# An encoder block on one core: output projection, norm 2 and feed-forward with features on the partitions and tokens along the free axis

## The chip, the cores and the metric

The kernel runs on one core of a Trainium2 chip. The metric is device time in microseconds (us) of one execution. The kernel before was run three times: median 1041.16 us, from 1040.82 to 1041.45. A profile of one execution shows what each engine did: TensorE (PE, and PEld for its weight loads), VectorE (DVE), ScalarE (ACT), GpSimd (POOL), and SyncE (SP), which issues most DMA transfers. Each engine works through its own queue in order; engines wait for each other through semaphores.

## What is computed

One layer of a transformer-like encoder on x of 1024 tokens by 1024 features, in float32:

```python
h = rms_norm(x, norm1_g)
z = h @ w_in
a, gate, q, k, v = jnp.split(z, splits, axis=-1)
conv_out = conformer_conv(a, gate, dw_kernel, dw_bias, conv_ln_g, conv_ln_b)
attn_out = neighbourhood_attention(rms_norm(q), rms_norm(k), v, rpb)
mix = jnp.concatenate([conv_out, attn_out], axis=-1)
x = x + mix @ w_out
h = rms_norm(x, norm2_g)
x = x + (jax.nn.silu(h @ w_gate) * (h @ w_up)) @ w_down
```

`w_out` is 1024 x 1024, `w_gate` and `w_up` are 1024 x 2816, `w_down` is 2816 x 1024. The tokens form a grid of 16 rows by 64 columns for the attention.

## The kernel before

A float32 product is made of three matmuls in a reduced format. `split` (L105) writes a high part with a cast on ACT (L106) and a low part, source less high part, on one or two engines that the caller names (L110: VectorE or POOL). `mac` (L112) then issues high by high, high by low, low by high. The first operand is the stationary one (the weight load, 128 by 128), the second the moving one (up to 512 columns).

*Weights of the output projection.* `want` lists the chunks, `issue` loads the next into one of three raw buffers (L148, tag R), `take` splits it (L151). `wo` comes as eight chunks of two 128-row blocks and 512 output features: wo04, wo06, wo00, wo02 for the first half of the features, wo14, wo16, wo10, wo12 for the second. All loads go through SP's queue in program order.

*Output projection.* `proj(t, d, acc, ks)` (L786) accumulates tile t of 128 tokens by half d of 512 output features over the eight blocks of the mixed features: blocks 4 to 7 come from attention (`at`), 0 to 3 from the convolution group (`cm`). The activations are stationary, the weights moving, so a result has tokens on the partitions and features along the free axis. After every `mac`, `weave` runs one piece of other work from the list `woven`. The first half of the features runs for tiles 0 to 5 in between the last attention blocks and the norm of the convolution group (L889 to L935), then for tiles 6 and 7 (L936 to L941). `take(2)` at L940 is where wo14 to wo12 are split. `resid` adds x to the result. The second half (L1204 to L1213) runs tile by tile; `norm2` stores the finished rows to the scratch `xd` in DRAM, sums the squares along the free axis with ACT (L948) and takes the root. One tile later `norm2_out` multiplies the rows by the reciprocal root and norm2_g (L956) into `xn`.

*From tokens to features.* The next products contract over features, so features must lie on the partitions. `t2_one` (L1198) transposes tokens 0 to 511 of `xn` with TensorE, four 128 x 128 transposes to a group (L1201), and splits the result into `h2`.

*Products with gate and up weights.* They are a Strassen-like scheme on 2 x 2 blocks: halves of the features and halves of the tokens on the left, pairs of weight blocks on the right. Seven products m1 to m7 stand in place of eight; `LEFT` (L1217) names the left operand of each: A11, A12, A22 are blocks of the normed x; S1 to S4 are sums of blocks, S1 = A21 + A22, S2 = S1 - A11, S3 = A11 - A21, S4 = A12 - S2. The left sums are made on the rows by `s_sum` (L1143), then transposed and split by `s_T` (L1157 to L1176), woven between the matmuls of the first products. A product is four `mac` of 512 columns for each of 22 pairs i of weight blocks (`product`, L1220); the weight sums are made by `t_sums` (L972), the operands by `prep` (L1106) and `part`. m1 and m2 accumulate in a bank A, m7 and m4 in D, m6, m5, m3 in B, and `evac` (L1237) reads a bank after each product, before the next product adds to it. Row pairs 0 and 1 run together, product by product, in the order of L984; the pairs from 2 on run in `ORDER` (L982). The results go to DRAM as operands of the next scheme (`keep`, L1269).

*Down products.* The seven products with `w_down` (L1437 to L1476) use the gated activations as the stationary operand and the weights as the moving one. `finish` adds the residual read back from `xd` (`load_res`, L1398) and `store` writes rows of the output.

Buffers: G tiles of 4 KB a partition (25), H tiles of 16 KB (6), R tiles for raw loads (3); PSUM has four banks `mm`, two `tp`, and `cv` of two banks.

## Time and profile before

| quantity | value |
|---|---|
| three runs, median (lowest to highest) | 1041.16 us (1040.82 to 1041.45) |
| the profiled execution, first to last instruction | 1039.2 us |
| mean granted TensorE clock | 0.999 |
| PE busy | 1033.1 us |
| DVE busy | 767.6 us |
| ACT busy | 477.5 us |
| POOL busy | 446.8 us |
| HBM read and written | 112.90 MB, 44.76 MB |

The span is that of one profiled execution; the runs' time also holds what lies around the first and last instruction. A row of the timeline has the start in us, the duration in us, engine, line, operation, out<-in by the program's names, the shape and a count; brackets at its end tell how long the engine sat idle before it and what ended that. SPq is a DMA issue on SP's queue. A row of the groups by tile has the number of instructions, then the shortest, the median and the longest duration in ns, and the first and last start. A row of the windows has the stretch and its length, then busy us and number of instructions for PE, PEld, DVE, ACT and POOL, the granted clock as a share of full speed, the DMA share and GB/s. The names in the rows leave buffer numbers out, so `t1m` is a weight operand of a product and `A`, `B`, `D` are the banks.

### The profile page before, as it was taken

What the parts mean: (1) busy time and instruction counts of PE and PEld (TensorE: products, weight loads), DVE (VectorE), ACT (ScalarE), POOL (GpSimd) and SP (SyncE); (2) the same over time, 40 slices, a digit from 0 to 9 for tenths busy, and PEclk for the clock granted to TensorE, in tenths of its full rate; (3) what the DMA queues carried; (4) which work ended last, traced back from release to release, by engine and by line L of the source; (5) the groups of instructions that cost most, each with busy time, mean ns of one, the idle gap of its engine ahead of it and who ended that gap; (6) DMA issues with size and microseconds to landing.
All of it is one profiled execution on the core that took longest, in us unless ns stands there. A gap on an engine that the chain in (4) does not pass through costs nothing.

```text
span 1039.2 us, 15251 instructions
## 1 busy us (share of the span) xinstructions
PE 1033.1 (99%) x5398; PEld 860.4 (83%) x5398; DVE 767.6 (74%) x1209; ACT 477.5 (46%) x1047; POOL 446.8 (43%) x351
## 2 busy tenths in 40 slices
PE   9999999999999999999999999999999999999998
PEld 7888888877777888888888888888888888888886
DVE  5788987886754257685888787787787767758884
ACT  7465348837866235434333334333342443433431
POOL 1036755524641302668776666667566200002310
PEclk9999999999999999999999999999999999999999
DMA  9426781247316422131434334424433597633741
GB/s 351 158 80 199 232 231 60 83 159 237 99 36 168 142 82 81 57 121 67 161 114 157 129 120 153 152 85 150 152 127 107 198 350 265 210 102 104 238 128 49
DMA packets 74077, 153.07 MB, mean 147 GB/s; under 512 B 13712, under 2 KB 22672, under 8 KB 73360
## 3 DMA queue, kind: packets, MB, share of 16 engines
q1 hardware_dynamic: 71984, 148.73, 43.3%
q10 hardware_dynamic: 2016, 3.35, 1.0%
q8 instruction: 43, 0.70, 0.3%
q14 instruction: 34, 0.28, 0.1%
HBM read 112.90 MB, written 44.76 MB: 152 GB/s over the span
## 4 chain that ended last, share of the span: by engine, by line
PE 98%; DVE 1%; ACT 1%; DMA 0%; issue 0%; DVEq 0%
PE B L114 6%; PE B L116 6%; PE B L115 6%; PE z L114 4%; PE z L115 4%; PE z L116 4%; PE D L114 4%; PE D L115 4%; PE D L116 4%; PE gl L116 3%; PE gl L114 3%; PE gl L115 3%; PE p L700 2%; PE o L719 2%; PE s L660 2%; PE pj L114 2%
## 5 line engine op out<-in xcount | busy, mean ns | idle before, releaser
L344 DVE SCALAR_TENSOR_TENSOR cv<-u,par,cv 128x1009 f32<-128x1009 f32 (+14 forms) x92 | 117.5, 1277 | 2.3
L370 POOL TENSOR_TENSOR pa<-pa,pr 128x1022 f32<-128x1022 f32 (+5 forms) x24 | 57.9, 2414 | 47.6 <-ACT pr L369 43.7
L106 ACT CAST op<-sr 128x512 fp32r<-128x512 f32 x77 | 47.7, 619 | 60.5 <-PE B2d L116 26.8
L1435 POOL TENSOR_TENSOR ou<-ou,resm 128x512 f32<-128x512 f32 x8 | 12.2, 1524 | 144.2 <-DMA resm<-xd 143.9
L110 DVE TENSOR_TENSOR op<-sr,op 128x512 fp32r<-128x512 f32 x77 | 59.3, 771 | 17.2 <-ACT op L106 17.2
L106 ACT CAST op<-wd 128x512 fp32r<-128x512 f32 x66 | 40.9, 619 | 29.9 <-DVE wd L1337 17.2
L689 POOL TENSOR_SCALAR e<-e,rs 128x288 f32<-128x288 f32 (+1 forms) x64 | 33.9, 545 | 42.0 <-DVE rs L687 41.8
L110 DVE TENSOR_TENSOR op<-wd,op 128x512 fp32r<-128x512 f32 x66 | 50.5, 765 | 1.5
L979 DVE TENSOR_TENSOR ts<-gu,ts 128x512 f32<-128x512 f32 x44 | 49.9, 1134 | 0.8
L678 ACT ACTIVATE e<-e,mx 128x288 f32<-128x288 f32 (+1 forms) x64 | 36.5, 571 | 18.8 <-DVE mx L673 18.8
L673 DVE CUSTOM_DVE_ANT_0 e<-s,tab 128x288 f32<-128x288 f32 (+1 forms) x64 | 28.7, 503 | 13.6 <-PE s L660 13.6
L1252 DVE TENSOR_TENSOR g<-D,g 128x512 f32<-128x512 f32 x22 | 15.2, 689 | 23.1 <-PE D L116 23.1
L1151 POOL TENSOR_TENSOR xn<-xn,xn 128x512 f32<-128x512 f32 x4 | 6.9, 1714 | 56.5 <-DVE sn L1151 50.9
L397 ACT ACTIVATE sq<-z,r 128x64 f32<-128x64 f32 x96 | 28.3, 329 | 4.5 <-PE z L116 4.5
L1259 ACT ACTIVATE D<-D 128x512 f32<-128x512 f32 x22 | 12.8, 582 | 35.8 <-DVE D L1258 35.8
L369 ACT ACTIVATE pr<-u,par 128x1022 f32<-128x1022 f32 (+5 forms) x24 | 27.0, 1137 | 1.6 <-ACT vs L427 1.6
L700 PEld LDWEIGHTS p<-ident,e 128*96 128x96 f32 (+1 forms) x192 | 20.6, 133 | 7.1 <-POOL e L689 6.3
L114 PE MATMUL B2d<-op 128*128 128x512 f32 x66 | 25.8, 391 | 0.0
L115 PE MATMUL B2d<-op 128*128 128x512 f32 x66 | 25.7, 389 | 0.0
L116 PE MATMUL B2d<-op 128*128 128x512 f32 x66 | 25.7, 389 | 0.0
L948 ACT ACTIVATE jk<-x 128x1024 f32<-128x1024 f32 x8 | 8.2, 1029 | 36.3 <-DVE x L841 36.3
L719 PE MATMUL o<-e,vw 96*64 96x128 f32 (+1 forms) x384 | 24.7, 277 | 0.0
(1479 smaller groups left out, 3748.7 us busy)
## 6 DMA issues: line engine op xcount, KB each, us to landing
gu<-in_gu SPq DMA_DIRECT2D x44, 512.0 KB
sr<-sd SPq DMA_DIRECT2D x77, 256.0 KB
sd<-sd SPq DMA_DIRECT2D x22, 512.0 KB
wd<-in_wd SPq DMA_DIRECT2D x44, 256.0 KB
sd<-g SPq DMA_DIRECT2D x33, 256.0 KB
x<-in_x SPq DMA_DIRECT2D x16, 512.0 KB
xd<-x SPq DMA_DIRECT2D x8, 512.0 KB
resm<-xd SPq DMA_DIRECT2D x16, 256.0 KB
```

Source lines behind the costliest of these rows:

```text
L106: act.copy(hi, src)
L110: eng.tensor_tensor(*[w[..., sl] for w in (lo, src, hi.bitcast(F32))], OP.subtract)
L114: pe.matmul(acc, lh, rh, start=start, stop=False, skip_group_check=True)
L115: pe.matmul(acc, lh, rl, start=False, stop=False, skip_group_check=True)
L116: pe.matmul(acc, ll, rh, start=False, stop=stop, skip_group_check=True)
L344: dve.scalar_tensor_tensor(acc[:, o], uc[:, i], dwk[:, c, t:t + 1], acc[:, o], OP.mult, OP.add)
L370: pool.tensor_tensor(pa[:, o], pa[:, o], pr[:, o], OP.add)
L678: act.activation(e, e, AF.Exp, bias=mx.pop((i, hh)), scale=-1.0, accum_out=sums[i][:, hh:hh + 1])
L689: pool.tensor_scalar(es[i][:, hh], es[i][:, hh], rs[:, hh:hh + 1], 1.0, op0=OP.mult, op1=OP.mult)
L700: pe.transpose(pt[:m, g * P:(g + 1) * P], es[i][:, hh, g * m:(g + 1) * m], ident)
L719: pe.matmul(os_[s_][hh * HD:(hh + 1) * HD, hp], vw[cb, rh + g][:, c:c + HD], pTs[i][hh][:, g], start=g == 0, stop=g == 2)
L979: dve.tensor_tensor(o, l, r, OP.subtract)
```

## The change

Everything from the output projection on has features on the partitions and tokens along the free axis.

- The host also lays out x as `xp`, features by tokens with the tokens in the order that the attention uses, and turns the output, now features by tokens, back. norm2_g becomes eight columns of `par`.
- `proj(m, h, ks, sel, every)` computes 128 output features m by 512 tokens h: weights stationary, activations moving. The first two units of the first token half run in two column pairs (`OUTER` and `INNER`), since the attention blocks finish in the order 0, 3, 1, 2. Units (0..3, 0) and (0..1, 1) come first, then (4..7, 0) and (2..7, 1).
- `at` lies in two H tiles; `wo` in pairs of G tiles except wo14 and wo16; some projection weights move from G to H; G has 21 tiles and H 7.
- `resid` adds x and stores to `xd` at once: sixteen stores of 256 KB in place of eight of 512 KB.
- Norm 2 sums over partitions: ACT squares each block, POOL adds the eight squares (`square`), TensorE multiplies by a column of ones (`token_sums`), ACT and VectorE take the root and the reciprocal, TensorE spreads it over partitions (`token_rows`), and VectorE scales each block in place (`norm2`).
- The transposes of `xn` and of the left sums go. `left` makes the left sums in place on the blocks, VectorE the sum, ACT the cast, POOL (for S2 VectorE) the low part. They are emitted after the products that the dictionary `after` names, and the order of the products of pairs 0 and 1 changes.
- For pairs 0 and 1, m4's gate and up steps follow m6 and m5 (`gate2`, `up2`). In the down products activations and weights change places.

The diff, cut to its core:

```diff
+        "xp": f["x"].reshape(2, 8, 4, 16, D).transpose(4, 0, 2, 3, 1).reshape(KB, P, S),
...
-        return T("G", [P, 1024], 25, name, dt)
+        return T("G", [P, 1024], 21, name, dt)
...
-        return T("H", [P, 4096], 6, name, dt)
+        return T("H", [P, 4096], 7, name, dt)
...
+            if (d, k0 // 4) == (1, 1):
+                if not woq:
+                    woq.append(H(f"wo{d}{k0}", F32R))
+                o = k0 % 4 * 1024
+                hl = (woq[0][:, o:o + 1024], woq[0][:, o + 1024:o + 2048])
+            else:
+                hl = (G(f"wo{d}{k0}h", F32R), G(f"wo{d}{k0}l", F32R))
...
+    xd = dr.tile([KB, P, S], F32, name="xd")
+    cm, xT, acc = [], {}, {}
+    OUTER, INNER = "outer", "inner"
+
+    def cols(w, sel):
+        if sel == OUTER:
+            return w.rearrange("p (b q) -> p b q", b=4)[:, 0:4:3]
+        return w[:, P:3 * P] if sel == INNER else w
+
+    def proj(m, h, ks, sel=None, every=1):
+        out = cols(acc[m, h], sel)
+        for n, k in enumerate(ks):
+            r = [cols((w[:, k] if k < 4 else w[:, k - 4])[:, h * 512:(h + 1) * 512], sel) for w in (cm if k < 4 else at)]
+            mac(out, [w[:, m % 4 * P:m % 4 * P + P] for w in wo[m // 4, k]], r, k == 4 and sel != INNER, k == 3)
+            if n % every == every - 1:
+                weave()
...
+    def load_xT(m):
+        xT[m] = G(f"xT{m}")
+        nc.sync.dma_start(xT[m], a["xp"][m])
+
+    def resid(m, h):
+        w = xT[m][:, h * 512:(h + 1) * 512]
+        dve.tensor_tensor(w, acc[m, h], w, OP.add)
+        nc.sync.dma_start(xd[m][:, h * 512:(h + 1) * 512], w)
+
+    def fill(m, *ks):
+        if not acc:
             act.activation(warm, eps, AF.Sqrt)
-            acc0.append(mm("pj0"))
-        proj(0, 0, acc0[0], ks)
+        if (m, 0) not in acc:
+            acc[m, 0] = mm(f"pj{m}0")
+        proj(m, 0, ks, OUTER)
...
-    fill(4, 5)
+    fill(0, 4, 5)
...
-    fill(7)
+    fill(1, 4, 5, 6, 7)
...
+    ATTN, CONV = (4, 5, 6, 7), (0, 1, 2, 3)
     take()
+    for m in range(2):
+        proj(m, 0, ATTN, INNER, 2)
     take()
+    for m in range(2, 4):
+        acc[m, 0] = mm(f"pj{m}0")
+        proj(m, 0, ATTN)
+    cc = cv("pj01")
+    acc[0, 1], acc[1, 1] = cc[:, :512], cc[:, 512:]
+    proj(0, 1, ATTN)
     act.activation(warm, eps, AF.Silu)
     conv_silu(0, 0)
+    proj(1, 1, ATTN)
+    for m in range(6):
+        load_xT(m)
     later = [(0, c) for c in range(1, 4)] + [(1, c) for c in range(4)]
     woven.extend(lambda q=q: conv_silu(*q) for q in later)
+    for h, ms_ in ((0, range(4)), (1, (0, 1))):
+        for k in CONV:
+            for m in ms_:
+                proj(m, h, (k,), None, 1 + (m + 1) % 2)
+        for m in ms_:
+            resid(m, h)
+        if h == 0:
+            take(2)
+    for m in range(6, 8):
+        load_xT(m)
+    take(2)
+    ssum, rn, rows = {}, {}, {}
+    def square(m, h, eng=pool):
+        sq = ST(f"sq2{m}{h}")
+        act.activation(sq, xT[m][:, h * 512:(h + 1) * 512], AF.Square)
+        if h not in ssum:
+            ssum[h] = sq
+        else:
+            eng.tensor_tensor(ssum[h], ssum[h], sq, OP.add)
+    def token_sums(h):
+        pt = tp(f"ss{h}")
+        for t in range(4):
+            pe.matmul(pt[:, t:t + 1], ssum[h][:, t * P:(t + 1) * P], one, start=True, stop=True)
+        sd, rn[h] = SM(f"r2{h}d", 4), SM(f"r2{h}r", 4)
+        act.activation(sd, pt[:, :4], AF.Sqrt, bias=eps, scale=1.0 / D)
+        dve.reciprocal(rn[h], sd)
+    def token_rows(h):
+        rows[h] = tp(f"rw{h}")
+        for t in range(4):
+            pe.transpose(rows[h][:, t * P:(t + 1) * P], rn[h][:, t:t + 1].to_broadcast([P, P]), ident)
+    def norm2(k, h):
+        w = xT[k][:, h * 512:(h + 1) * 512]
+        dve.scalar_tensor_tensor(w, w, g2[:, k:k + 1], rows[h], OP.mult, OP.mult)
...
-    products = [(i, p) for p in ("m1", "m2", "m6", "m5", "m7", "m4", "m3") for i in range(2)]
+    products = [(i, p) for p in ("m1", "m2", "m7", "m4", "m6", "m5", "m3") for i in range(2)]
...
+            if i > 1 and p == ("m6" if parted(i, "m1") else "m1"):
                 t_sums(i, (1, 2))
-            elif p == ("m7" if parted(i, "m1") else "m6"):
+            elif i > 1 and p == ("m7" if parted(i, "m1") else "m6"):
...
+    sop = {}
+    h2 = [H(f"h2{w}", F32R).rearrange("p (k s) -> p k s", s=512) for w in range(2)]
+    def block(r, k):
+        return xT[k % HK + HK * (r[1] == "2")][:, 512 * (r[0] == "2"):512 * (r[0] == "2") + 512]
+    def left(n, k, sub=pool):
+        if n not in sop:
+            q = H(n, F32R).rearrange("p (w k s) -> p w k s", w=2, s=512)
+            sop[n] = [[q[:, h, i] for i in range(HK)] for h in range(2)]
+        o, l, r, op = {"S3": ("21", "11", "21", OP.subtract), "A22": ("22", "22", "22", None),
+                       "S2": ("22", "22", "21", OP.subtract), "S1": ("11", "22", "11", OP.add),
+                       "S4": ("12", "12", "22", OP.subtract)}[n]
+        if op is not None:
+            dve.tensor_tensor(block(o, k), block(l, k), block(r, k), op)
+        split(sop[n][0][k], sop[n][1][k], block(o, k), (sub,))
+    def h2_one(k):
+        norm2(k, 0)
+        split(h2[0][:, k], h2[1][:, k], xT[k][:, :512])
...
+    units = [(m, 0) for m in range(4, 8)] + [(m, 1) for m in range(2, 8)]
+    for m in range(4):
+        square(m, 0)
+    beside = {(2, 5): [lambda: token_sums(0)], (3, 1): [lambda: token_rows(0)],
+              (4, 5): [lambda: t_sums(0, (1, 2))], (5, 5): [lambda: t_sums(0, (3, 4))],
+              (7, 3): [lambda: t_sums(1, (1, 2))], (7, 5): [lambda: t_sums(1, (3, 4))]}
+    for kb, at_ in enumerate(((3, 3), (3, 7), (4, 3), (4, 7), (5, 3), (5, 7), (6, 3), (6, 7))):
+        beside.setdefault(at_, []).append(lambda kb=kb: h2_one(kb))
+    for m, h in units:
         for n in range(KB):
+            woven.append(lambda fs=beside.get((m, n), ()) if h else (): [f() for f in fs])
+        acc[m, h] = mm(f"pj{m}{h}")
+        proj(m, h, ATTN + CONV)
         unravel()
+        resid(m, h)
+        square(m, h, pool if (m, h) != (7, 1) else dve)
+        if (m, h) == (4, 0):
+            for t in range(2):
+                square(t, 1)
+        if h == 1 and m in (3, 4, 5, 6):
             prep()
...
+    def gate2(i, acc):
+        dve.tensor_tensor(acc, acc, u2[i], OP.add)
+        act.activation(acc, acc, AF.Silu)
+
+    def up2(i, r, acc):
+        dve.tensor_tensor(r, acc, r, OP.mult)
+        keep(i, 1, r)
...
             dve.tensor_tensor(u2[i], acc, l, OP.add)
+            if i < 2:
+                gate2(i, bank[i, "D"])
...
-            dve.tensor_tensor(r, acc, l if (p == "m5") == (i < 2) else r, OP.add)
+            dve.tensor_tensor(r, acc, l if p == "m7" else r, OP.add)
+            if i < 2 and p == "m5":
+                up2(i, r, bank[i, "D"])
...
+    after = {0: lambda: (token_sums(1), act.activation(warm, eps, AF.Silu)),
+             1: lambda: [(norm2(k, 1), left("S3", k)) for k in range(HK)],
+             2: lambda: [(norm2(k + HK, 1), left("A22", k)) for k in range(HK)],
+             3: lambda: [left("S2", k, dve) for k in range(HK)],
+             5: lambda: [left("S1", k) for k in range(HK)],
+             7: lambda: [left("S4", k) for k in range(HK)]}
     for n, (i, p) in enumerate(products):
-        if i == 0 and p in NEXT:
-            s_weave(NEXT[p])
-        acc = product(i, p)
-        for t in {3: (0, 1, 2, 3), 6: (4,), 7: (5,), 8: (6,), 9: (7,)}.get(n, ()):
-            s_sum(t % 4, (3 + t // 4,), pool)
-        evac(i, p, acc)
-        if n == 0:
-            norm2_out(7)
-            act.activation(warm, eps, AF.Silu)
-            s_sum(3, (1, 2), dve)
+        if n == 1:
+            woven.extend([lambda: None, lambda: token_rows(1)])
+        pacc = product(i, p)
+        evac(i, p, pacc)
+        if n in after:
+            after[n]()
...
-            prep({3: 2, 5: 3}.get(n, 0))
+            prep((1, 1, 1, 1, 1, 1)[n])
...
-        nc.sync.dma_start(res[p, t], xd[(4 * tok + t) * P:(4 * tok + t + 1) * P, d * 512:(d + 1) * 512])
+        nc.sync.dma_start(res[p, t], xd[4 * d + t][:, tok * 512:(tok + 1) * 512])
...
+        o += tok * 512
+        (queue or (nc.scalar if p == "m4" else nc.sync)).dma_start(a["out"][4 * d + t][:, o:o + w.shape[-1]], w)
...
-        mac(acc, [q[:, h, t * P:(t + 1) * P] for h in range(2)], [q[:, 2 + h] for h in range(2)],
+        mac(acc, [q[:, 2 + h, t * P:(t + 1) * P] for h in range(2)], [q[:, h] for h in range(2)],
...
+    out = r.results[0]["out_0_dram"].reshape(D, 2, 4, 16, 8)
+    return np.ascontiguousarray(out.transpose(1, 4, 2, 3, 0)).reshape(1, S, D)
```

More of the change, by code (lines that the diff above doesn't have):

```diff
@@ L182, in g_pair, with quad, dst @@
         return dst
+    def quad(name, into):
+        held, n = [], [0]
+        def dst():
+            if not held:
+                held.append(H(name, F32R))
+            o = n[0] * 2048
+            n[0] += 1
+            hl = (held[0][:, o:o + 1024], held[0][:, o + 1024:o + 2048])
+            into.append(hl)
+            return hl
+        return dst
     wn = {n: [] for n in range(3)}
     wag = {(i, c): [] for i in range(2) for c in range(4)}
+    wkq, w0q = quad("wkq", wn[1]), quad("w0q", wn[0])
     for k2 in range(4):
-        want(a["qkv"][1, k2], f"wk{k2}", g_pair(f"wk{k2}", wn[1]), (dve, pool))
+        want(a["qkv"][1, k2], f"wk{k2}", wkq if k2 < 2 else g_pair(f"wk{k2}", wn[1]), (dve, pool))
     for c in range(4):
@@ L720, in weigh, with at_of, evac_lo @@
                           start=g == 0, stop=g == 2)
+    def at_of(s_):
+        rh, cb = order[s_]
+        o = rh * 512 + cb * P
+        return [w[:, :, o:o + P] for w in at]
     def evac_hi(s_):
[L723 to L731 removed]
+        if not at:
+            at.extend(H(f"at{w}", F32R).rearrange("p (k s) -> p k s", s=S) for w in range(2))
+        act.copy(at_of(s_)[0], os_[s_])
+    def evac_lo(s_):
+        hi, lo = at_of(s_)
+        dve.tensor_tensor(lo, os_[s_], hi.bitcast(F32), OP.subtract)
     def value(t):
@@ L1469, in build @@
     for half in range(2):
-        acc, cols = GB[half][:, :256], slice(half * 256, half * 256 + 256)
+        acc, part_ = GB[half][:, :256], slice(half * 256, half * 256 + 256)
         for k in (QF - 2, QF - 1):
             q = ops[(len(SEQ) - 1) * QF + k]
-            mac(acc, [q[:, h, 3 * P:] for h in range(2)], [q[:, 2 + h, cols] for h in range(2)], k == QF - 2, k == QF - 1)
-        w = quarter(om["u"], 0, 3)[:, cols]
+            mac(acc, [q[:, 2 + h, 3 * P:] for h in range(2)], [q[:, h, part_] for h in range(2)], k == QF - 2, k == QF - 1)
+        w = quarter(om["u"], 0, 3)[:, part_]
         dve.tensor_tensor(w, acc, w, OP.add)
```

181 lines of the change are left out of this document (22 added, 159 removed).

## The prediction

> **What bounds the kernel now.** I read the header of the page and the chain that ended last first, then the granted clock, then windows cut at the milestones of TensorE around the change.
>
> ```profile
> span 1039.2 us, 15251 instructions
> PE 1033.1 (99%) x5398; PEld 860.4 (83%) x5398; DVE 767.6 (74%) x1209; ACT 477.5 (46%) x1047; POOL 446.8 (43%) x351
> PE 98%; DVE 1%; ACT 1%; DMA 0%; issue 0%; DVEq 0%
> ```
>
> TensorE sets the end: it is busy for 99% of the span and holds 98% of the chain. So what leaves TensorE's queue comes off the time one to one, and any new wait in its queue goes onto it one to one. The stages that change, by windows (busy us of each engine, then granted clock, DMA share, GB/s):
>
> ```profile
> 342.88:353.76 10.88, 10.88 (x50) 9.01 (x48) 1.98 (x3) 1.05 (x1) 5.26 (x3) 1.00 0.83 280
> 353.76:401.39 47.63, 47.47 (x225) 39.09 (x224) 25.30 (x38) 16.96 (x33) 3.38 (x2) 1.00 0.23 87
> 401.39:449.76 48.37, 48.27 (x250) 39.32 (x248) 35.79 (x52) 24.51 (x43) 24.71 (x19) 1.00 0.14 46
> 449.76:535.00 85.24, 85.24 (x421) 72.12 (x419) 65.88 (x88) 30.91 (x60) 66.07 (x49) 1.00 0.39 131
> ```
>
> They are: tiles 6 and 7 of the first output half; the second half with norm 2; the products of row pairs 0 and 1 with the left sums (14 products); then the steady products. The first row gives the pitch of a 128x512 matmul: 48 weight loads in 10.88 us, 0.2267 us each. A `mac` is 0.68 us, a product of 12 matmuls is 2.72, a unit of 24 is 5.44. At 0.2267 the 192 matmuls of the second row need 43.5 us and the 168 of the third 38.1; the rest there is transposes.
>
> **What leaves.** The transposes, by tile:
>
> ```profile
> L1201 PE MATMUL t<-ident,xn x32: 270/272/328, 381.0 to 397.2; 128*128 128x128 f32 x32
> L1170 PE MATMUL sq<-ident,xn x24: 270/272/328, 422.9 to 439.9; 128*128 128x128 f32 x24
> L1170 PE MATMUL sq<-ident,sn x20: 270/272/275, 410.7 to 417.4; 128*128 128x128 f32 x20
> L1170 PE MATMUL sp<-ident,xn x24: 270/272/273, 426.6 to 442.1; 128*128 128x128 f32 x24
> L1170 PE MATMUL sp<-ident,sn x12: 272/272/273, 413.7 to 420.1; 128*128 128x128 f32 x12
> ```
>
> They make 112, or 28 groups of four. One group's price, from its neighbours:
>
> ```profile
> 410.46 0.40 PE L116 MATMUL A<-h,t1m 128*128 128x512 f32 x1
> 410.70 0.60 PE L1170 MATMUL sq<-ident,sn 128*128 128x128 f32 x4
> 411.06 0.47 PE L114 MATMUL A<-h,t1m 128*128 128x512 f32 x1
> 411.37 0.39 PE L115 MATMUL A<-h,t1m 128*128 128x512 f32 x1
> ```
>
> From 410.46 to 411.37 there are two matmuls and a group: 0.91 - 0.45 = 0.46 us. So 28 x 0.46 = 12.9 us leave TensorE.
>
> **What TensorE gains.** The multiplies stay the same in number, with weights and activations exchanged. Units 0 and 1 of the first token half are computed in column pairs, 48 matmuls of 256 columns for 24 of 512:
>
> ```profile
> 535.25 0.28 PE L115 MATMUL q60m<-h,qa6m 128*128 128x256 f32 x1
> 535.37 0.28 PE L116 MATMUL q60m<-h,qa6m 128*128 128x256 f32 x1
> ```
>
> The pitch is 0.12, so 48 x 0.12 - 24 x 0.2267 = +0.3 us. `token_sums` and `token_rows` are four small matmuls each, twice: at the group price 4 x 0.46 = 1.8 (bounds 0.9 and 3.7, half and double). Ten units then stand between 342.88 and the first product: 240 matmuls, 54.4 us.
>
> With no wait, TensorE's work from 342.88 to the end of the 14 products is 54.4 + 38.1 + 0.3 + 1.8 = 94.6 us, where 106.9 passed before (449.76 - 342.88; its own 1.5 us of waits included): **-12.3 us**. Everything now depends on the waits.
>
> **Wait 1: the last output weights.** The stores of x to `xd` are issued in `resid`, and for the first four units these now stand in SP's queue ahead of the loads of wo10 and wo12.
>
> ```profile
> 314.70 0.37 SPq L148 DMA_DIRECT2D wo10r<-in_wo  x1
> 341.07 0.37 SPq L148 DMA_DIRECT2D wo12r<-in_wo  x1
> 345.08 1.05 ACT L106 CAST wo<-wo12r 128x1024 fp32r<-128x1024 f32 x1 [4.64 <-DMA wo12r<-in_wo]
> 343.34 2.41 POOL L110 TENSOR_TENSOR wo<-wo10r,wo 128x1024 fp32r<-128x1024 f32 x1
> 346.21 2.39 POOL L110 TENSOR_TENSOR wo<-wo12r,wo 128x1024 fp32r<-128x1024 f32 x1 [0.46 <-ACT wo L106]
> 338.24 2.48 DVE L841 TENSOR_TENSOR x<-pj,x 128x512 f32<-128x512 f32 x4
> ```
>
> Before, wo10 was asked for at 314.7. After, it waits for the four stores, whose residual adds end at 340.7, so it is issued near 341.1 and wo12 near 341.5. The row of wo12 shows 4.0 us from issue to use: landing near 345.2 and 345.9. Cast 1.05 and low part 2.4 give wo10 near 348.7; POOL's next 2.4 gives wo12 near 351.1. Before, the first use was at 353.76, behind two tiles that used the first half's weights. After, unit (4,0) starts at 343.2 and uses them from its fifth block: 343.2 + 2.7 + 0.2 = 346.1 for wo10's low part. Stall 2.6, then two blocks (1.4), then 1.0 for wo12: about **4.0** (3 to 6, since the loads share the queues with four stores of 256 KB). Nothing fills it: the unit is in order. First product T0 = 342.9 + 0.3 + 54.4 + 0.9 + 4.0 = 402.5, where it was 401.39.
>
> **Waits 2 to 4: VectorE and POOL in the products.** Four rows decide their prices:
>
> ```profile
> 456.37 1.74 POOL L110 TENSOR_TENSOR t2m<-gu,t2m 128x512 fp32r<-128x512 f32 x1
> 456.88 1.78 DVE L1052 TENSOR_TENSOR qtm<-qtm,qtm 128x512 f32<-128x512 f32 x1
> 486.24 0.69 DVE L1252 TENSOR_TENSOR g<-B,g 128x512 f32<-128x512 f32 x1 [2.36 <-PE B L116]
> 486.24 1.29 POOL L1047 TENSOR_TENSOR qtm<-h,h 128x512 f32<-128x512 f32 x1
> ```
>
> Two operations with two SBUF inputs, one on each engine, don't overlap: VectorE's takes 1.78 where 0.69 is its length, POOL's 1.74 where it is 1.29. With an input in PSUM (third row) VectorE isn't held. So a pair of such operations on both engines costs about 1.74 us.
>
> The Trainium skill, "GPSIMD Engine Reference", section "8. Key points", states this contention for VectorE instructions with two SBUF inputs; the rows agree (0.69 against 1.78). It speaks against this change, which trades TensorE's transposes for such operations on both engines.
>
> The casts and small operations at T0:
>
> ```profile
> 407.56 0.30 ACT L950 ACTIVATE r27d<-s,eps 128x1 f32<-128x1 f32 x1
> 407.88 1.28 ACT L1365 ACT_TABLE_LOAD   x1
> 407.89 0.16 DVE L954 RECIPROCAL r27r<-r27d 128x1 f32<-128x1 f32 x1 [0.95 <-ACT r27d L950]
> 411.39 0.59 ACT L106 CAST S<-sq 128x512 fp32r<-128x512 f32 x1 [0.68 <-PE sq L1170]
> ```
>
> *Wait 2, S3.* The second half's token sums follow the first product (2.7 + 0.5), then 0.3, 0.16 and the rows: norm 2 of the half starts near T0+5.2. ACT loads a table and copies A1 first, so the cast of S3's block 0 ends near T0+7.7. POOL then makes four low parts at 1.3 to 1.74 each, and m7's right operand for i=1. TensorE reaches m7 at T0 + 4 x 2.72 + 0.9 = T0+11.8 and leaves it, unhindered, at T0+17.3; POOL lets it go at 18.6 to 20.4. Taken: **2.0** (0 to 3).
>
> *Wait 3, bank D of m7.* m4 is accumulated into m7's bank after VectorE has read it. `evac` of m7 stands in VectorE's queue behind the eight operations of `left("S2")`: a subtraction and a low part for each of four blocks. Each subtraction overwrites A22's block, so it waits for POOL's low part of A22; each low part waits for ACT's cast. POOL ends A22's first low part near T0+17.2. A block takes 0.69 + 0.75 + 0.69 = 2.1 us alone and near 3.0 with POOL busy on the next low parts. So the evacuation ends near 17.2 + 4 x 3.0 + 0.7 = T0+29.9; TensorE is ready at T0+19.3. Taken: **10.6**. Lower bound: POOL's A22 free at 16.2, 4 x 2.1 + 0.7, so T0+25.3 against 18.6: 6.7. Upper: 12.5. Queued behind it on TensorE is everything; m6, whose operand S2 is made just then, is behind m4.
>
> *Wait 4, bank B of m6.* m5 is accumulated into B after VectorE made u2 from it. Ahead of that in its queue are 13 operations: two evacuations and low parts, four sums of S1, four of S4. TensorE is ready four products after T0+29.9, at T0+40.8. Alone the 13 take 9 us and hide. Meanwhile POOL has four low parts of S1, a sum for a part, four of S4: nine pairs at 1.74 with five alone end near T0+49. As half of POOL's wait for sums not made yet, I take the middle: **5.0** (0 to 8).
>
> *Clock.* Such idle stretches cost speed too:
>
> ```profile
> 1034.84 0.28 PE L116 MATMUL B1d<-op 128*128 128x256 f32 x1
> 1036.00:1037.50 1.50, 0.00 (x0) 0.00 (x0) 0.00 (x0) 0.00 (x0) 0.00 (x0) 1.00 0.91 270
> 1037.50:1039.20 1.70, 0.00 (x0) 0.00 (x0) 0.00 (x0) 0.00 (x0) 0.00 (x0) 0.68 0.11 34
> 1.04 3.62 PE L255 MATMUL up<-ones 128*128 128x128 f32 x18 [1.04 <-POOL ones L251]
> ```
>
> About 3 us after the last matmul the granted clock falls (0.68 over a window that began full). From cold, 18 matmuls of 128 columns take 3.62; at a quarter of 0.46 they would take 2.07. A restart loses about 1.5. Wait 3 is long enough, waits 1 and 4 hardly: **1.5** (0 to 4.5). The Trainium skill, "TensorE: Matmul & The Clock Gate", "Part 1: The HAM clock gate (the "warmup" mystery)", has full rate back after about 3.4 us of activity; by it the loss would be an estimated 1.7, as half of 3.4 is lost. The trace agrees on the fall.
>
> One more: `ts` of i=2 stands ahead of g1's evacuation on VectorE and waits for a load that POOL's late m3 operand holds up: **0.5** (0 to 1).
>
> Covered at nothing: norm 2 of the first half (eight low parts of 1.29 on POOL, eight multiplies on VectorE) lies beside 43 us of units, in a stage where POOL was busy 3.4 of 47.6 us; uncovered it would cost up to 10. The sixteen stores of 256 KB are eight of 512 KB before; the down products exchange operands of the same shape, and their rows and stores keep their sizes.
>
> **Sum.** -12.3 + 4.0 + 2.0 + 10.6 + 5.0 + 1.5 + 0.5 = +11.3 us on the profiled span of 1039.2: 1050.5. The runs' median, 1041.16, lies 2.0 above that span: **1052.5 us**. Own range, with the distances to the bounds added as squares (low: 1, 2, 3.9, 5, 1.5 make 6.9; high: 2, 1, 1.9, 3, 3 make 5.2): 1046 to 1058.
>
> **Rivals.**
> A, covered. Every wait is hidden, TensorE's saving stays: 1041.2 - 12.3 = 1028.9. For it: the chain is 98% TensorE. Against: no cover of 25 us is seen for VectorE's order. Chance 0.06.
> B, the other side: VectorE and POOL don't hold each other in this chain, because each low part waits for a cast and they seldom meet. Its place is wait 3 and it decides from 12.3 us of waits down. Waits 3.0 (weights) + 1.0 (S3) + 6.7 (D) + 0 + 1.0 (clock) = 11.7, less 12.3: 1040.6. For it: VectorE has 12 us to spare in the third window. Against: 456.37. Chance 0.13, about half of it faster and half the same.
> C, worse: POOL holds VectorE at every operation of waits 3 and 4, so that these and the clock reach their upper bounds together (+1.9 + 3.0 + 3.0): 1060.4. Against: much of POOL's work there waits for sums that VectorE has still to make. Chance 0.08.
> Forecast: 0.73.
>
> Faster by over 0.2% (2 us, what these runs can tell): A and some of B, 0.12. Same 0.06. Slower 0.82. Range 1040 to 1061.
>
> **What would show it.** In the profile after: the first product near 402.5, not 398.5; the idle before `pj` of unit 4 put down to wo10 and wo12; a gap near 10 us before m4's first matmul, put down to VectorE's evacuation of D; one of some 5 before m5, by u2; granted clock under 1.00 behind the first; i=2 starting near 460. Wrong would be: VectorE's S2 operations at 0.69 beside POOL, no gap at D, or a stage after i=2 longer than before.

## The result, and the profile after

Four runs of the kernel after the change have a median of 1057.23 us (1055.64 to 1057.52), four of the kernel before 1041.17. The ratio is 1.0152, 95% interval 1.0138 to 1.0167: the change costs 16 us. Three of the four runs had a mean granted TensorE clock of 0.988 and took 1057.08 to 1057.52 us, the fourth 0.992 and 1055.64, so runs of one kernel differ by up to 1.9 us. The profiled execution, one of the three, has a span of 1055.7 us, 16.5 more than before.

The page's header and the chain that ended last, after the change:

```profile
span 1055.7 us, 15166 instructions
PE 1031.6 (98%) x5334; PEld 859.2 (81%) x5334; DVE 777.8 (74%) x1200; ACT 477.6 (45%) x1044; POOL 490.5 (46%) x380
PE 88%; DVE 7%; ACT 2%; POOL 1%; issue 1%; DMA 1%; DVEq 0%; ACTq 0%; POOLq 0%
```

TensorE's share of the chain fell from 98% to 88%, and VectorE took 7%. PE's busy time is only 1.5 us less than before although 112 transposes are gone; 6.5 us of it are matmuls that a slower clock stretched, as shown below. The windows at the same milestones as before (the units of the projection, then the 14 products; columns as before):

```profile
344.03:403.65 59.62, 56.73 (x253) 46.09 (x252) 22.74 (x30) 19.46 (x31) 34.06 (x24) 1.00 0.33 120
403.65:466.74 63.09, 47.00 (x182) 37.10 (x180) 47.74 (x54) 24.02 (x43) 40.83 (x29) 0.81 0.10 34
```

The products took 48.37 us before and take 63.09 now; TensorE idles in 16 of them and runs at a granted clock of 0.81. VectorE's work in this stage rose from 35.79 to 47.74, POOL's from 24.71 to 40.83. Behind the stage nothing changed: from the first product of pair 2 to the end it is 589.0 us now (1055.7 - 466.74) and was 589.4. What TensorE waited for from 340 to 470 us, by the view of the waits (us in total, times, longest):

```profile
PE D L115 <- DVE g L1258: 10.1, 1, 10.1
PE B L115 <- DVE u L1249: 4.2, 1, 4.2
PE pj L117 <- POOL wo10l L111: 1.7, 1, 1.7
PE ss L978 <- DVE sq L973: 1.2, 1, 1.2
PE pj L117 <- POOL wo12l L111: 0.7, 1, 0.7
PE B L115 <- ACT t2m L107: 0.5, 1, 0.5
PE pj L115 <- ACT wo10h L107: 0.5, 1, 0.5
```

All but one of these were named ahead: the weights (0.5 + 1.7 + 0.7), bank D, bank B, and a last one, which the row puts down to ACT; VectorE's read of B for pair 1, behind the sums that wait for the load of pair 2, ended at 463.8, and TensorE went on at 463.93. The wait at the token sums wasn't named. VectorE's timeline shows how D came about:

```profile
423.40 1.76 DVE L1179 TENSOR_TENSOR xT<-xT,xT 128x512 f32<-128x512 f32 x1 [2.33 <-POOL A L111]
425.85 0.99 DVE L111 TENSOR_TENSOR S<-xT,S 128x512 fp32r<-128x512 f32 x1 [0.68 <-ACT S L107]
426.76 1.74 DVE L1179 TENSOR_TENSOR xT<-xT,xT 128x512 f32<-128x512 f32 x1
429.19 0.99 DVE L111 TENSOR_TENSOR S<-xT,S 128x512 fp32r<-128x512 f32 x1 [0.68 <-ACT S L107]
430.10 0.68 DVE L1179 TENSOR_TENSOR xT<-xT,xT 128x512 f32<-128x512 f32 x1
...
433.44 0.69 DVE L111 TENSOR_TENSOR S<-xT,S 128x512 fp32r<-128x512 f32 x1 [0.68 <-ACT S L107]
434.05 0.68 DVE L1258 TENSOR_TENSOR g<-D,g 128x512 f32<-128x512 f32 x1
```

POOL's timeline at the same place:

```profile
427.92 1.71 POOL L111 TENSOR_TENSOR t0m<-ts,t0m 128x512 fp32r<-128x512 f32 x1
434.01 1.27 POOL L111 TENSOR_TENSOR t1m<-ts,t1m 128x512 fp32r<-128x512 f32 x1 [4.38 <-ACT t1m L107]
```

VectorE waits for POOL's low part of A22, then makes S2: a sum, a wait of 0.68 for ACT's cast, a low part, four times over. The first two sums take 1.76 and 1.74 us while POOL works, the third takes 0.68 while POOL is idle (429.63 to 434.01). Only then does it read D, whose product had ended some 12 us before. TensorE then restarts slowly (timeline of the first matmuls of m4, and the clock around it in windows):

```profile
434.88 0.77 PE L115 MATMUL D<-A,t0m 128*128 128x512 f32 x1 [10.12 <-DVE g L1258]
435.45 0.63 PE L116 MATMUL D<-A,t0m 128*128 128x512 f32 x1
435.87 0.63 PE L117 MATMUL D<-A,t0m 128*128 128x512 f32 x1
```

```profile
425.00:426.00 1.00, 0.00 (x0) 0.00 (x0) 0.32 (x2) 0.62 (x1) 1.00 (x1) 1.00 0.00 0
426.00:427.00 1.00, 0.00 (x0) 0.00 (x0) 1.00 (x2) 0.00 (x0) 1.00 (x2) 0.85 0.00 0
427.00:428.00 1.00, 0.00 (x0) 0.00 (x0) 1.00 (x1) 0.00 (x0) 1.00 (x2) 0.50 0.00 0
...
439.00:440.00 1.00, 1.00 (x4) 0.81 (x3) 0.92 (x1) 0.05 (x1) 1.00 (x2) 0.50 0.05 16
440.00:441.00 1.00, 1.00 (x5) 0.78 (x5) 0.00 (x0) 1.00 (x3) 1.00 (x1) 0.82 0.00 0
```

The pitch is 0.43 instead of 0.2267, and m4's first product lasts 5.26 us (434.88 to 440.14) instead of 2.72.

### The profile page after: what moved, and what is told of

Same layout as the page of the kernel before. It is cut to its first block, busy times and chain, and to the rows that moved or that the text cites. A ratio compares the mean times of both kernels' runs of the same rounds, so it can differ in the third digit from the quotient of the medians.

```text
span 1055.7 us, 15166 instructions
## 1 busy us (share of the span) xinstructions
PE 1031.6 (98%) x5334; PEld 859.2 (81%) x5334; DVE 777.8 (74%) x1200; ACT 477.6 (45%) x1044; POOL 490.5 (46%) x380
## 4 chain that ended last, share of the span: by engine, by line
PE 88%; DVE 7%; ACT 2%; POOL 1%; issue 1%; DMA 1%; DVEq 0%; ACTq 0%; POOLq 0%
PE B L115 5%; PE B L116 5%; PE B L117 5%; PE z L115 4%; PE z L117 4%; PE z L116 4%; PE D L115 3%; PE D L116 3%; PE D L117 3%; PE gl L115 3%; PE gl L117 3%; PE gl L116 3%; PE p L720 2%; PE o L739 2%; PE s L680 2%; PE pj L117 2%
## 5 line engine op out<-in xcount | busy, mean ns | idle before, releaser
L107 ACT CAST op<-wd 128x512 fp32r<-128x512 f32 x54 | 33.4, 619 | 29.1 <-DVE wd L1345 18.5
L111 DVE TENSOR_TENSOR op<-wd,op 128x512 fp32r<-128x512 f32 x54 | 41.3, 764 | 1.2
L867 DVE TENSOR_TENSOR xT<-pj,xT 128x512 f32<-128x512 f32 x16 | 10.6, 685 | 28.3 <-PE pj L117 28.3
L973 POOL TENSOR_TENSOR sq<-sq,sq 128x512 f32<-128x512 f32 x13 | 18.1, 1394 | 17.0 <-ACT sq L969 16.7
L115 PE MATMUL B2d<-op 128*128 128x512 f32 x66 | 25.8, 391 | 0.0
```

The source lines that it names most:

```text
L107: act.copy(hi, src)
L111: eng.tensor_tensor(*[w[..., sl] for w in (lo, src, hi.bitcast(F32))], OP.subtract)
L115: pe.matmul(acc, lh, rh, start=start, stop=False, skip_group_check=True)
```

## The experiments

Each was timed in turn with the kernel before on the same chip, which gives the ratios; medians are also compared with 1057.23 for the kernel after.

**Stores behind the weight loads.**

```diff
         dve.tensor_tensor(w, acc[m, h], w, OP.add)
-        nc.sync.dma_start(xd[m][:, h * 512:(h + 1) * 512], w)
+        if (m, h) not in [(j, 0) for j in range(4)]:
+            keep_x(m, h)
...
         if h == 0:
             take(2)
+            for m in ms_:
+                keep_x(m, h)
```

> The four stores of the first units are issued behind the loads of wo10 and wo12; nothing else moves. If the stores ahead of the loads are what made the output projection wait: wo10 is asked for near 315 as before the change, wo12 still waits for its raw buffer (POOL's low part of wo14, to 342.2) and is cast near 347 and split near 349.8, so of the 2.9 us of waits in unit (4,0) about 1.3 stay, the first product starts near 402 (403.65 after the change), and the time falls by 1.5 to 2.5 us, to about 1055. Rival, the products' waits absorb any earlier start because VectorE's queue sets them: the first product is earlier, the time within 0.5 us of 1057.2.

1053.35 us (1052.84 to 1054.54), ratio 1.0121 (1.0106 to 1.0136). SP's timeline, first of the kernel after, then of this run:

```profile
340.12 2.11 SPq L868 DMA_DIRECT2D xd<-xT  x4
342.32 0.41 SPq L149 DMA_DIRECT2D wo10r<-in_wo  x1
342.79 0.49 SPq L149 DMA_DIRECT2D wo12r<-in_wo  x1
```

```profile
318.48 0.38 SPq L149 DMA_DIRECT2D wo10r<-in_wo  x1
341.78 0.38 SPq L149 DMA_DIRECT2D wo12r<-in_wo  x1
```

wo10 is asked for 24 us earlier, wo12 one; only 1.1 us of waits are left, for wo12. The first product starts at 400.80 instead of 403.65, and the whole stage behind it moves with it: m4 still waits 10.1 us, m5 4.2. So the wait was what the prediction said, and this gain isn't absorbed. Its size is less sure: the two profiled runs, both at a granted clock of 0.988, lie 2.8 us apart (1054.54 against 1057.38), their spans 2.9, the medians 3.9. All are above the 1.5 to 2.5 that were expected.

**VectorE's order alone: D is read before S2 is made.**

```diff
-             3: lambda: [left("S2", k, dve) for k in range(HK)],
-             5: lambda: [left("S1", k) for k in range(HK)],
+             5: lambda: [left("S2", k, dve) for k in range(HK)],
+             6: lambda: [left("S1", k) for k in range(HK)],
```

> S2 is made after both evacuations of m7, S1 after m4's first product; nothing else moves. If VectorE's order alone makes the wait of 10.1 us at bank D: the wait goes and the time falls by 10 us or more (with the clock that it costs). If POOL's rate stands right behind it: m4's right operand t0m4 is the tenth low part in POOL's queue and ends near 429.6, so a wait of about 5 us stays, put down to POOL, and the time falls by 4 to 7 us, to 1050 to 1053.

1056.63 us (1056.06 to 1057.38), ratio 1.0151 (1.0136 to 1.0167): no change. Its waits on TensorE:

```profile
PE B L115 <- DVE u L1249: 11.2, 1, 11.2
PE D L117 <- POOL t0m L111: 4.5, 1, 4.5
```

Both expectations were wrong. The wait at D went from 10.1 to 4.5 and is POOL's, as the second said, but what was gained there came back at bank B, where u2 was made at 452.7 to 453.4, no earlier than before (452.0 to 452.7). Moving a wait along TensorE's queue gains nothing while VectorE and POOL need as long up to u2.

**The clock alone.** Spare matmuls keep TensorE busy where it idled; nothing that they compute is used.

```diff
+    def idle_mm(n):
+        w = cv("idle")[:, :512]
+        for _ in range(n):
+            pe.matmul(w, h2[0][:, 0, :P], h2[0][:, 0, :512], start=True, stop=True)
...
+        if h:
+            idle_mm(5)
         pt = tp(f"ss{h}")
...
+        if n in (6, 10):
+            idle_mm({6: 40, 10: 26}[n])
```

> Extra matmuls into a spare bank fill TensorE's idle time: 5 ahead of the second half's token sums, 40 ahead of m4's first product, 26 ahead of m5's first. No wait is taken away. The granted clock should then stay near 1.00 through the stage. If the losses of the clock simply add up (1.7 + 2.5 + 2.3 us measured behind the three idle stretches): the time falls by about 6.5 us, to 1050.7. If VectorE sets when m4 and m5 may start, what is saved behind D is lost again as a longer wait at B: only the loss behind B and a part of the first are saved, 2 to 3.5 us, to about 1054.

1056.78 us (1055.14 to 1057.83), ratio 1.0151 (1.0134 to 1.0168): no change, and both expectations missed. The window of the stage shows that the spare matmuls did their work, a clock of 1.00 instead of 0.81:

```profile
403.44:466.06 62.62, 57.43 (x252) 45.60 (x251) 48.07 (x54) 24.25 (x43) 41.56 (x29) 1.00 0.10 34
```

m4 and m5 run at full speed (the first products of each take 2.8 us), yet the stage is 62.62 us instead of 63.09. What m4 saved is lost waiting for u2. What m5 saved is lost at m3, and VectorE's timeline shows to what:

```profile
451.30 0.68 DVE L1256 TENSOR_TENSOR u<-B,g 128x512 f32<-128x512 f32 x1
452.01 0.70 DVE L1241 TENSOR_TENSOR D<-D,u 128x512 f32<-128x512 f32 x1
...
458.95 1.87 DVE L1014 TENSOR_TENSOR ts<-gu,gu 128x512 f32<-128x512 f32 x1 [2.30 <-DMA gu<-in_gu]
460.86 1.63 DVE L1014 TENSOR_TENSOR ts<-gu,ts 128x512 f32<-128x512 f32 x1
462.42 0.68 DVE L1265 TENSOR_TENSOR g<-B,g 128x512 f32<-128x512 f32 x1
```

After u2 comes a chain that has nothing of TensorE in it: the gate on ACT, behind it ACT's cast of m3's weights, POOL's low part, then the load of pair 2 (issued at 455.3), VectorE's sums of it, and only behind those B of pair 1, which m3 needs (463.24). So in the kernel after, the 6.5 us that the slow clock costs TensorE (below) lie beside other waits; worth having is 0.5 of them.

**Low parts on VectorE.** POOL's 16 low parts of A22, S1, S3, S4 move to VectorE, one block behind the sums so that ACT's casts are covered; S2 is done likewise. The order of S2 ahead of D is kept.

```diff
-        split(sop[n][0][k], sop[n][1][k], block(o, k), (sub,))
+        hi, lo = sop[n][0][k], sop[n][1][k]
+        act.copy(hi, block(o, k))
+        return lambda: dve.tensor_tensor(lo, block(o, k), hi.bitcast(F32), OP.subtract)
+
+    def lefts(n, h=None):
+        low = []
+        for k in range(HK):
+            if h is not None:
+                norm2(k + h, 1)
+            low.append(left(n, k))
+            if k:
+                low.pop(0)()
+        low.pop(0)()
```

> All low parts of the left sums are made by VectorE, one block behind the sums so that ACT's casts are hidden; the order of S2 ahead of m7's evacuation stays. If VectorE and POOL hold each other at two SBUF inputs, VectorE alone is faster than both: its operations there take 0.69 instead of up to 1.77, D is evacuated near 432 instead of 434, the chain from D to u2 takes 14.5 us instead of 18, the wait at B shrinks from 4.2 to about 1 and the clock behind it holds: 1049 to 1052. If they don't, VectorE has 12 more operations of 0.69 in its queue (A22, S1, S3, S4 have four each, 16 in all) and the time rises by 5 us or more.

1050.47 us (1050.10 to 1051.31), ratio 1.0093 (1.0078 to 1.0108): 6.8 us faster with 16 more operations in VectorE's queue. Its window of the stage, and TensorE's waits:

```profile
404.11:460.62 56.51, 43.95 (x182) 35.06 (x181) 47.72 (x70) 24.25 (x43) 16.46 (x12) 0.91 0.11 37
```

```profile
PE D L115 <- DVE g L1270: 8.0, 1, 8.0
PE B L115 <- DVE u L1261: 1.9, 1, 1.9
```

VectorE does 70 operations in the busy time in which it did 54 before (47.72 against 47.74 us), because POOL no longer works beside most of them. D is read at 432.2, as expected. The first theory holds: two-input operations of both engines hold each other, and POOL's 16 low parts saved VectorE nothing. As its busy time is the same, the gain lies in its idle time, 8.8 us of the stage instead of 15.4. In the kernel after, VectorE stands still for 7.5 us between norm 2 and u2 (2.3 for POOL's low part of A22, 5.1 for ACT's casts); in this run it goes through without a gap. How much of that the order one block behind would give by itself was not tried.

**Both: low parts on VectorE and the later order** (S2 after product 5, S1 after 6, S4 after 9).

> As the run with all low parts on VectorE, and also S2 after both evacuations of m7, S1 after m4's first product, S4 after m6's second. With the low parts on POOL the order alone gained nothing. If VectorE's queue from norm 2 to u2 is now the bound (it was busy without a gap from 412.4 to 449.9 in the run before): m4 waits about 2 us instead of 8, u2 of pair 0 is made near 441 instead of 447.8, since S4's eight operations no longer stand ahead of it, and the next pair starts near 456 instead of 460.6: 1045 to 1048. If the sum of VectorE's work alone counts, the waits only move once more: within 1 us of 1050.5.

1050.29 us (1049.94 to 1050.43), ratio 1.0087 (1.0070 to 1.0104): the same as without the order. The first expectation was wrong, the rival right. u2 of pair 0 was made at 441.2, as expected, and m4 waited 2.3 us, but m3 and the next pair started hardly earlier:

```profile
403.67:459.31 55.64, 44.86 (x182) 33.99 (x180) 50.78 (x70) 24.35 (x43) 16.92 (x12) 0.94 0.11 38
```

VectorE is busy for 50.78 of 55.64 us, 91% of the stage. It is nearly the bound there, and the two orders tried within its queue only chose which product waits.

**The token sums woven in.** The sums and rows stand two blocks later, between matmuls of the second product.

```diff
-    after = {0: lambda: (token_sums(1), act.activation(warm, eps, AF.Silu)),
-             1: ...
+    def sums1():
+        token_sums(1)
+        act.activation(warm, eps, AF.Silu)
+
+    after = {1: ...
...
-            woven.extend([lambda: None, lambda: token_rows(1)])
+            woven.extend([lambda: None, sums1, lambda: None, lambda: token_rows(1)])
```

> The kernel after the change, with the second half's token sums two blocks later, between the matmuls of the second product, and their rows two blocks after that. TensorE no longer idles before the sums (1.2 us) and the clock should not fall there. If VectorE's chain from norm 2 on sets the end of the stage: the rows come about 1 us earlier (409.5 instead of 410.5, norm 2 from 410.0 instead of 411.6) and the time falls by 1 to 2 us, less than the 2.9 us that TensorE saves at that place. If TensorE's own time counts: 3 us less.

1055.86 us (1055.65 to 1058.01), ratio 1.0145 (1.0129 to 1.0160), 1.4 below the kernel after, with overlapping runs: inconclusive by its time. In the trace the wait at the sums is gone, the rows come at 409.75 instead of 410.49, and the waits at D and B are 10.2 and 5.4: part of TensorE's gain went into a longer wait at B, as the first expectation has it. The stage is 1.5 us shorter (61.63 against 63.09), within the 1 to 2 expected.

**Later stores, low parts on VectorE with the later order, and woven sums together.**

> All of it together: stores behind the weight loads (3.9 us gained alone), low parts on VectorE with the later S2, S1 and S4, and the sums woven in. If these act on different links of one chain their gains add up: 1046.5 - 3.9 - 1.5, about 1041, level with the kernel before the change (1040.8). If the load of the third pair's weights is the next link, it stays 2 to 4 us above that.

1046.16 us (1046.09 to 1046.25), ratio 1.0047 (1.0032 to 1.0062). Better by 11 us than the change as made, slower by 5 than the kernel before, and 5 above the first expectation. Most of this miss is its base: it took 1046.5 for the run before, which came to 1050.29. The two edits added here gain 4.1 together. In the traces the first product starts 3.05 us earlier (400.62 against 403.67), which is the stores' part, and the stage is 0.8 shorter (54.85 against 55.64), which leaves the sums about half of the 1.5 that they gave alone. The second expectation's cause is wrong: no load is waited for. Waits of 2.3 (D), 4.2 and 2.6 us (B) stay, all by VectorE.

**One attempt to shorten VectorE's operations further**: POOL's sums for the later quarter products of m1 moved behind the 14 products, weight operands made three products ahead instead of four.

```diff
-    TOK = {6: (tok_full, "m1", 0), 8: (tok_full, "m1", 3), 9: (tok_full, "m1", 2), 10: (tok_full, "m1", 1),
+    TOK = {6: (tok_full, "m1", 0), 13: (tok_full, "m1", 1), 14: (tok_full, "m1", 3), 15: (tok_full, "m1", 2),
...
-            prep(upto=n + 4)
+            prep(upto=n + (4 if n > 12 else 3))
```

> The run with all edits together, and also POOL's sums for the later quarter products of m1 behind the first 14 products instead of among them, and each weight operand made three products ahead instead of four. Both take two-input operations away from beside VectorE's. If VectorE is the bound and POOL's neighbours lengthen its operations (S4's first two took 3.5 us instead of 1.3), 2 to 3 us are gained: about 1043.5. If not, no change from 1046.2.

1055.19 us (1054.93 to 1056.75), ratio 1.0138 (1.0122 to 1.0153): a failure. Pair 2 did start 1.1 us earlier (454.41 instead of 455.47), but the moved sums were then late themselves, and TensorE waited for an operand made of them behind the stage:

```profile
PE q41m L116 <- POOL qT2m L111: 5.0, 1, 5.0
PE B L115 <- DVE g L1277: 1.5, 1, 1.5
```

**What the transposes cost.** The kernel before, with every group of transposes issued twice:

```diff
-        for j in range(1 + two):
+        for j in [*range(1 + two)] * 2:
...
-        for i in range(4):
+        for i in [0, 1, 2, 3] * 2:
```

> The kernel before the change, with each of the 28 groups of four transposes issued twice. It prices the work that the change takes from TensorE. If a group costs TensorE 0.46 us on the path that sets the end: 28 times that, 12.9 us more, 1054. If the transposes stand partly in idle time that something else makes, or gain by running back to back: less, 6 to 10 us more.

1051.65 us (1051.39 to 1051.99), ratio 1.0101 (1.0086 to 1.0116): 10.5 us more, 0.38 a group, between the two expectations. The second group of a pair runs right behind the first, without a switch from and to 512-column matmuls: eight in a row span 0.80 us to the next matmul.

```profile
399.33 1.04 PE L1201 MATMUL t<-ident,xn 128*128 128x128 f32 x8
400.13 0.47 PE L114 MATMUL pk<-wo,at 128*128 128x512 f32 x1
```

The second group adds 0.34 us there (0.80 less the 0.46 of a group alone), 9.5 for all 28. The run lost no less, so none of it was hidden, and the change does take about 10 to 13 us of work from the bound.

**Without the left sums.** Two runs leave them out to see what TensorE would need. The first makes neither A22 nor S1 to S4; the products read A11.

> The kernel after the change without the left sums: A22 and S1 to S4 are not made, and the products that use them read the block A11 instead; norm 2 of both halves stays. VectorE loses 16 sums and 4 low parts, POOL 16 low parts, ACT 20 casts; TensorE's work is the same. If these operations alone make the products' stage long, what is left is TensorE's 38.1 us with the sums and rows of norm 2 and their idle time, some 43 us instead of 63.1: the time falls by about 20 us, to 1036 to 1038, below the kernel before. If something else (the loads of weights, the clock) would hold the stage anyway, it falls by less than 15 us.

1045.35 us (1045.11 to 1046.55), ratio 1.0043 (1.0027 to 1.0060): 11.9 us below the kernel after, less than the 15 that the second expectation set. The stage itself fell from 63.1 to 41.2 us (403.98 to 445.20), a little more than expected, but TensorE then waited elsewhere, between 460 and 500:

```profile
PE B L116 <- POOL h L111: 5.9, 1, 5.9
PE B L115 <- ACT h L107: 1.4, 1, 1.4
```

In the program a later quarter operand is written into the buffer of A11, `h2`, which the products of this run read up to then. So this wait comes from the run's own edit, and only its stage says something of the change. The second run makes A22, leaves out only S1 to S4, and lets the products read A22:

```diff
+             1: lambda: [(norm2(k + HK, 1), left("A22", k)) for k in range(HK)],
+             2: lambda: [norm2(k, 1) for k in range(HK)]}
...
+        if n == 2:
+            sop.update({q: sop["A22"] for q in ("S1", "S2", "S3", "S4")})
```

> The kernel after the change without S1 to S4: A22 is made from norm 2's blocks, and the products that use S1 to S4 read A22. Unlike the run that read A11, no later work overwrites what they read. VectorE loses 16 sums and 4 low parts, POOL 12 low parts. If that work is what the stage waits for: the stage takes 41 to 43 us instead of 63.1 and, with nothing new behind it, the time falls by 20 to 22 us, to about 1036. If it falls by less than 15 us again, some later stage gives back what this one gains.

1036.46 us (1035.94 to 1037.21), ratio 0.9955 (0.9939 to 0.9972): 20.8 us below the kernel after, as expected. The stage takes 41.2 us (404.33 to 445.53), at a clock of 1.00 and with no wait but the 1.2 us at the token sums. A window around it:

```profile
403.65:446.00 42.35, 41.10 (x187) 33.61 (x186) 25.56 (x35) 14.60 (x27) 21.87 (x18) 1.00 0.15 50
```

> The same without S1 to S4, and with the stores behind the weight loads and the token sums woven in. Every wait that the trace shows is then gone but 1.1 us for wo12. If the change's saving on TensorE is all there and only VectorE's late work hides it: 1036 less 3.9 less 1.2 to 2.9, 1029.5 to 1031, against 1028.9 for the case in which everything is covered. If not, it stays above 1034.

This adds the later stores and the woven sums: 1031.47 us (1031.18 to 1031.97), ratio 0.9906 (0.9891 to 0.9921), 0.5 above the upper expectation, with one wait left in the stretch, 1.2 us for wo12. The saving on TensorE is there: 9.9 us against the kernel before (1041.32 beside this run), with that 1.2 still waited for. Between this run and the kernel after lie 25.8 us. 20.8 of them are the left sums S1 to S4 of the second token half, made late by VectorE and POOL; 5.0 are the early stores and the token sums.

## Why the prediction came out as it did

The direction and the cause were right: TensorE's saving, 12.3 us by the forecast and 9.9 to 10.5 by the runs, was more than eaten by waits. The time, 1057.2, lay 4.7 us above the forecast of 1052.5 and 0.8 below the upper end of its own range, 1058. Step by step, against the profiled execution:

| step | forecast | measured |
|---|---|---|
| first unit behind the weights starts | 343.2 | 344.03 |
| wait 1, added to that unit | 4.0 | 3.8 (9.21 us instead of 5.44) |
| first product T0 | 402.5 | 403.65 |
| norm 2 of the second half starts | T0+5.2 | T0+7.9 |
| wait 2, S3 | 2.0 | none |
| D evacuated | T0+29.9 | T0+31.1 |
| wait 3, bank D | 10.6 | 10.1 |
| wait 4, bank B | 5.0 | 4.2 |
| m5 starts | T0+45.8 | T0+49.2 |
| lost to the clock | 1.5 | 6.5 (1.7 + 2.5 + 2.3) |
| next pair starts | 461.1 | 466.74 |

Two rows of the forecast are worked out from the prediction: m5 starts at T0+40.8 and the wait of 5.0, the next pair at 449.76 and the sum of +11.3.

The mechanism of wait 1 is shown by the run with the later stores, and that of waits 3 and 4 by those without the sums: they vanish with the sums and only move when the order changes. That the two engines hold each other is shown by the run with VectorE alone; the length of a pair, about 1.74, is in the rows above (1.74 and 1.76).

Three terms were mis-sized. *The clock*: the two long restarts took 2.5 and 2.3 us from a product, not 1.5, and with the short one (1.7) there were three instead of one. The 1.7 that was estimated from the rule in the Trainium skill, "TensorE: Matmul & The Clock Gate", "Part 1: The HAM clock gate (the "warmup" mystery)", was nearer: right for the short one, too small for the long ones. *Wait 2* was nothing, because the idle time before the token sums and the slow clock behind them held TensorE back long enough. *The start of norm 2*: the sums waited 1.2 us for the last square, and the rows then ran at half clock, so that VectorE's chain began 2.7 us late. I had walked that link with no wait in it. That wait 3 still came out at 10.1 for 10.6 is partly luck: VectorE began S2 2.6 us later than forecast (423.40, T0+19.8 instead of T0+17.2), took 2.7 us a block instead of 3.0, and TensorE was itself ready 1.8 us later (T0+21.1 instead of T0+19.3), so the errors largely cancelled.

The step that failed in kind is the addition of the clock to the waits. The run with spare matmuls gave the clock back and gained 0.5 us by its median, no more than the spread of the runs. The sum should have followed VectorE instead: its chain from norm 2 to u2, then the load of pair 2. The bounds that I gave wait 4 (0 to 8) contain this, but I priced it as TensorE's wait, which hangs on when TensorE gets there; the time at which u2 is made does not. It was T0+48.3 to 49.0, near my upper bound for that chain (T0+49), as POOL held VectorE at most of the operations (up to 1.77 us where 0.69 is their length) and VectorE waited twice 1.2 us for ACT's casts.

Rival A, all covered, is 1031.5 once the sums are gone, against 1028.9. Rival B asked that the engines don't hold each other; they do. What the forecast called covered held: the stretch behind the stage is 0.5 us shorter than before.

Why the layout makes this work late was not tried by itself, but it stands in the code: with tokens on the partitions each tile of 128 tokens was normed as soon as it was finished, and most sums for S1 and S2 were made beside the projection. With features on the partitions no token of the second half has its norm before the last of eight units, so 8 multiplies, 16 sums and 20 low parts come at once, in front of products that need them.

## What to carry to other kernels

When a change takes work from the busiest engine, lay out the queue of the next engine in the stage that follows and sum its operations, at the lengths that they take beside the other engines. Here VectorE's 47.7 us stood against 38.1 of TensorE's products, and neither of the two other orders tried brought the saving back. A wait on the bound engine isn't a price by itself; follow the queue that ends it to the last thing that it releases, because time given back in between (order, clock, an idle gap) was here mostly waited out later. A layout that needs all of a norm's inputs before its first output turns work that was spread out into work at one point.

## What had not been expected of the hardware

- POOL's low parts beside VectorE's operations cost VectorE as much as making them itself: with 16 more of them in its queue, and POOL busy 16.5 instead of 40.8 us, VectorE's busy time in the stage stayed at 47.7 us.
- The granted clock fell 1.9 and 2.0 us after the end of the last matmul in the two long idle stretches (424.8 to 426.7, 448.6 to 450.6) and came back 5.5 and 4.6 us after the restart (434.88 to 440.4, 452.82 to 457.4). In the kernel after it also fell at 409.6, behind only 1.2 us of idle and eight matmuls of one column, which together lasted 2.5 us from the last wide matmul to the next, and came back at 413.1. The same idle, 1.2 us, in the run with low parts on VectorE and the later order brought no fall: its four transposes for the rows take 0.60, not 1.06.
- These changes, read from windows of 1 us, lie on a grid: 409.64, 413.06, 426.70, 440.36, 450.60 and 457.42 are 3.42, 13.64, 13.66, 10.24 and 6.82 us apart, which is 1, 4, 4, 3 and 2 times 3.41. So the loss at a restart hangs on where it lies on the grid, and a short gap can cost a step in one execution and none in another. Wait 1 brought no fall in the kernel after (clock 1.00 from 346 to 354) and one in the run with spare matmuls (0.50 from 350 to 352).

The four transposes, first of the kernel after, then of the run with the later order:

```profile
410.49 1.06 PE L986 MATMUL rw<-ident,r21r 128*128 128x128 f32 x4
```

```profile
410.11 0.60 PE L986 MATMUL rw<-ident,r21r 128*128 128x128 f32 x4
```
